# Transposes of query and key tiles in pairs at written places, one product group later

## The chip, the cores and the metric

One core of a Trainium2 chip runs the whole layer in one launch. The metric is the device time of an execution in microseconds. Before the change the median of three runs is 989.9 us (989.79 to 989.96). Five parts of the core matter here: TensorE multiplies matrices and transposes tiles; VectorE and ScalarE do elementwise work, and they alone take results out of PSUM, the memory that TensorE writes; GpSimd and SyncE issue transfers.

## The reference

One decoder layer on 256 tokens of width 2048. Three mixers work on one projection of the normed input and are joined by an output product; a gated feed-forward part follows. The change touches the second mixer, attention with low-rank queries and keys (8 heads, 128 plain and 64 rotary channels for each query and key, values of 128):

```python
q = (rms_norm(q_lat, g_q_lat) @ w_q_up).reshape(B, S, MLA_HEADS, MLA_QK_DIM)
kv = (rms_norm(kv_lat, g_kv_lat) @ w_kv_up).reshape(B, S, MLA_HEADS, MLA_NOPE_DIM + MLA_V_DIM)
k_nope, v = kv[..., :MLA_NOPE_DIM], kv[..., MLA_NOPE_DIM:]
...
q = rms_norm(q, g_q_mla)
k = rms_norm(k, g_k_mla)
q = jnp.concatenate([q[..., :MLA_NOPE_DIM], apply_rope(q[..., MLA_NOPE_DIM:], pos)], axis=-1)
k = jnp.concatenate([k[..., :MLA_NOPE_DIM], apply_rope(k[..., MLA_NOPE_DIM:], pos)], axis=-1)
o = causal_attention_blocks(q, k, v)
```

## The kernel before

Every fp32 operand of a large product is split into a rounded high part (ScalarE, L103, `wh`) and the rest (VectorE, L104, `wl`), and three products of these parts stand for one. The splits go through four buffers each, so a cast waits until TensorE has finished with the split four before it.

The stretch in question is the up-projection. `pool_in(g)` multiplies one group of the pooling mixer's channels, 48 matmuls of 256 columns (L134). `q_up(n)` gives the queries: n = 2 the rotary parts of all heads, n = 0 and 1 the plain parts of heads 0 to 3 and 4 to 7, 24 matmuls of 512 columns each (L185 to L187). `kv_up(0)` gives the keys in two halves of 12 such matmuls (h = 0: heads 0 to 3, h = 1: heads 4 to 7), `kv_up(1)` the values in two halves. These products have tokens on the partitions, in two tiles of 128 tokens (`tt`). The scores need features on the partitions, so each query or key tile (128 x 512) goes a way of its own: out of PSUM by ScalarE (L651 queries, L656 rotary queries, L686 keys) into a `tok` buffer of three; its squares and their sums (L272, L273) for the norm; for the rotary queries six operations of VectorE (L636 to L638); for the keys the norm's factor (L688, L212, L213, L691, L692) and a multiplication (L693); then `to_features`, four transposes on TensorE (L279) into a PSUM bank and a copy out of it (L283 and L287 on ScalarE, L285 on VectorE). Ten such tiles make ten sets of four transposes: two of rotary queries, four of keys, four of plain queries.

The code calls pool groups and up-projections in turn: `pool_in(0)`, `q_up(2)`, `pool_in(1)`, `kv_up(0)`, `pool_in(2)`, `q_up(0)`, `pool_in(3)`, `q_up(1)`, `kv_up(1)`. A scheduler then sets the order of instructions on every engine; only instructions given to `keep()` hold the order in which they are written among themselves. The transposes of L279 aren't given to it, so the scheduler puts them between the products where it takes them to be ready.

After that comes the output product (`out_part`), 24 matmuls of 512 columns a part, with steps of the attention in between: `mla_steps()` is called after every six matmuls (1.36 us at 0.227 us each) and counts its calls in `done[0]`. At call 1 the rotary keys are transposed (`rope_keys`, L727), at call 3 the pooling mixer's last product and the scores of heads 0 and 1 are made, and from call 6 on, every fourth call, the values of the head before, the turn of a head's probabilities (`turn`, three transposes, L495) and the scores of the head two further on (L742). Beside that, `first_jobs` makes sums of blocks of the down-projection's weights (subtractions L546 on VectorE, loads L539 and stores L548 by GpSimd).

Of the kernel before, what the change touches and what calls it, by code (L numbers as in the profile page):

```python
# [11 lines left out]
F32 = mybir.dt.float32  # L12
# [6 lines left out]
P = 128  # L19
# [4 lines left out]
H = 8  # L24
# [41 lines left out]
def layer(ctx, tc, xT_d, xn_d, memT_d, vec_d, tab_d, w_z_d, w_mqkr_d, w_q_d, w_kv_d, w_mem_d, w_pool_d, w_o_d,  # L66
          w_g_d, w_u_d, w_dn_d, out_d):
    nc = tc.nc
# [8 lines left out]
    def nm(s):  # L77
        uid[0] += 1
        return f"{s}_{uid[0]}"

    def ps_main():
        return psm.tile([P, 512], F32, tag="m", name=nm("psm"))

    def ps_aux():
        return psa.tile([P, 512], F32, tag="a", name=nm("psa"))

    def load_w(src, n, cut=STG, kept=False):
        raw = stage.tile([P, STG], F32, tag="wr", name=nm("wr"), bufs=3)
        for c in range(0, n, cut):
            keep(nc.sync.dma_start(raw[:, c:min(n, c + cut)], src[:, c:min(n, c + cut)]), kept)  # L90
        return raw[:]

    def keep(ins, on=True):

        return tc.keep_in_program_order(ins) if on else ins
# [45 lines left out]
    def gemm_z(ps, raw, act, between, low_first):  # L141


        nk = HS // P
        parts = [split_w(raw, c * HS, HS, shift=16 if c else 48) for c in range(KD // nk)]
        for low in ((True, False) if low_first else (False, True)):
            for k in range(KD):
                i = k % nk
                for a, m in enumerate(rounds(act, k, low)):
                    keep(nc.tensor.matmul(ps, parts[k // nk][low][:, i * P:(i + 1) * P], m,  # L150
                                          start=k + a == 0 and low == low_first,
                                          stop=k == KD - 1 and low != low_first, skip_group_check=True))
            if low == low_first:
                between()
# [62 lines left out]
    mp = mix.enter_context(tc.tile_pool(name="mix", bufs=1))  # L217

    identf = mp.tile([P, P], F32, name="identf")
# [11 lines left out]
    def sm(n):  # L231
        o = so[0]
        so[0] += n
        return small[:, o:o + n]

    def tok():
        return mp.tile([P, 512], F32, tag="tok", name=nm("tok"), bufs=3)
# [30 lines left out]
    def head_sq(dst, src):  # L268

        sq = mp.tile([P, 512], F32, tag="hsq", name=nm("hsq"), bufs=2)  # L270
        s3 = sq[:, :src.shape[1] * src.shape[2]].rearrange("p (h d) -> p h d", h=src.shape[1])
        nc.scalar.activation(s3, src, AF.Square)  # L272
        nc.vector.tensor_reduce(dst, s3, axis=AX.X, op=ALU.add)  # L273

    def to_features(dst, src, tt, n, scale=None, eng=None, bank=ps_aux):

        ps = bank()
        for i in range(n):
            nc.tensor.transpose(ps[:, i * P:(i + 1) * P], src[:, i * P:(i + 1) * P], identf[:])  # L279
        d = dst[:, :, tt * P:(tt + 1) * P]  # L280
        p3 = ps[:, :n * P].rearrange("p (i t) -> p i t", t=P)
        if scale is not None:
            nc.scalar.activation(d, p3, AF.Copy, scale=scale)  # L283
        elif eng == "v":
            nc.vector.tensor_copy(d, p3)  # L285
        else:
            nc.scalar.copy(d, p3)  # L287
# [29 lines left out]
    ps = ps_aux()  # L317
# [25 lines left out]
    for c in range(KD // 2):  # L343
# [10 lines left out]
        if c % 2:  # L354
            h = slice(2 * c - 2, 2 * c + 2)
# [5 lines left out]
    ps = ps_aux()  # L361
# [23 lines left out]
    gqk = sm(2)  # L385
# [137 lines left out]
    def mem_steps(m):  # L523
        if m == 0:
            mq_done()
        for h, step in beside.get(m, ()):
            (mem_heads[h].score, mem_heads[h].turn, mem_heads[h].values)[step]()
        if m == 6:
            latent_scales()
# [25 lines left out]
    for m in range(6):  # L555
        raw = load_w(w_z_d[m], STG)
        ps = ps_main()[:, 0:T]
        gemm_z(ps, raw, xg, lambda: mem_steps(m), m % 2 == 1)
        a = zs[:, m // 4, :]
        if m % 4 == 0:  # L560
            nc.scalar.activation(a, ps, AF.Square)
        else:
            t = mp.tile([P, T], F32, tag="zsq", name=nm("zsq"), bufs=2)
# [23 lines left out]
    def pool_in(g):  # L587
        raw = load_w(w_z_d[6 + g], STG)
        ps = ps_main()[:, 0:T]
        gemm_z(ps, raw, xg, lambda: mem_steps(6 + g), False) if g == 0 else gemm_t(ps, raw, 0, xg, range(KD))  # L590
        nc.vector.tensor_tensor(zp[:, g, :], ps, rxb[:], op=ALU.mult)
        if g % 2:
            keep(nc.sync.dma_start(x1n[:, g // 2, :], xn_d[g // 2]))
# [28 lines left out]
    qnT, knT, krT, qrT = qkv[:, 0:8], qkv[:, 8:16], qkv[:, 16:24], mqT  # L622
# [6 lines left out]
    def rotate(dst, src, s, tt, nh):  # L629
# [5 lines left out]
        for a, b, (ra, rb), op, o in ((x1, x2, (r[0], r[1]), ALU.subtract, 0), (x2, x1, (r[2], r[3]), ALU.add, 32)):  # L635
            nc.vector.tensor_tensor(t[:, 0], a, ra, op=ALU.mult)  # L636
            nc.vector.tensor_tensor(t[:, 1], b, rb, op=ALU.mult)
            nc.vector.tensor_tensor(dst[:, :, o:o + 32], t[:, 0], t[:, 1], op=op)  # L638

    def q_up(n):  # L640
        raw = load_w(w_q_d[n], STG)
        pss = [[ps_main()[:]] for _ in range(NT)]
        for i in range(2):
            hi, lo = split_w(raw, i * HS, HS)
            gemm_n(pss, hi.rearrange("p (k n) -> p k n", n=512), lo.rearrange("p (k n) -> p k n", n=512),
                   zl, 2 * i, i == 0, i == 1)
        for tt in range(NT):
            ps = pss[tt][0]
            t = tok()
            if n < 2:  # L650
                nc.scalar.copy(t[:], ps)  # L651
                head_sq(ssq_n[:, tt, 4 * n:4 * n + 4], t[:].rearrange("p (h d) -> p h d", d=NOPE))
                to_features(qnT[:, 4 * n:4 * n + 4], t, tt, 4, gqk[:, 0:1])
            else:
                t1 = tok()
                nc.scalar.copy(t1[:], ps)  # L656
                p3 = t1[:].rearrange("p (h d) -> p h d", d=ROPE)
                head_sq(ssq_r[:, tt, :], p3)
                rotate(t[:].rearrange("p (h d) -> p h d", d=ROPE), p3, 0, tt, H)
                to_features(qrT, t, tt, 4)  # L660

# [3 lines left out]
        head_sq(sskr[:, tt:tt + 1], kr[:, tt:tt + 1, :])  # L667
        rotate(krr[:, tt], kr[:, tt:tt + 1, :], 1, tt, 1)
    nc.vector.tensor_tensor(sskr, sskr, rx2, op=ALU.mult)
    def kv_up(n):  # L670
        raw = load_w(w_kv_d[n], STG)
        for h in range(2):
            pss = [[ps_main()[:]] for _ in range(NT)]
            hi, lo = split_w(raw, h * HS, HS)
            gemm_n(pss, hi.rearrange("p (k n) -> p k n", n=512), lo.rearrange("p (k n) -> p k n", n=512),
                   zl, 4, True, True)
            for tt in range(NT):
                ps = pss[tt][0]
                p3 = ps.rearrange("p (h d) -> p h d", d=128)
                if n == 1:  # L680
                    nc.scalar.activation(vv[:, tt, 4 * h:4 * h + 4, :], p3, AF.Copy, scale=skv[:, tt:tt + 1])
                    continue
                t = tok()
                t3 = t[:].rearrange("p (h d) -> p h d", d=NOPE)
                o = slice(tt * H + 4 * h, tt * H + 4 * h + 4)
                nc.scalar.copy(t[:], ps)  # L686
                head_sq(fk[:, o], t3)
                nc.vector.tensor_scalar(fk[:, o], fk[:, o], skv2[:, tt:tt + 1], sskr[:, tt:tt + 1],  # L688
                                        op0=ALU.mult, op1=ALU.add)
                rsqrt_(fk[:, o], fk[:, o], 1.0 / QK)  # L690
                nc.vector.tensor_scalar(fkn[:, o], fk[:, o], skv[:, tt:tt + 1], None, op0=ALU.mult)  # L691
                nc.vector.tensor_scalar(fkr[:, o], fk[:, o], rx[:, tt:tt + 1], None, op0=ALU.mult)  # L692
                nc.vector.tensor_tensor(t3, t3, fkn[:, o].unsqueeze(2).to_broadcast([P, 4, NOPE]), op=ALU.mult)  # L693
                to_features(knT[:, 4 * h:4 * h + 4], t, tt, 4, None, "v")


    pool_in(0)
    q_up(2)
    pool_in(1)
    kv_up(0)  # L700
    pool_in(2)
    q_up(0)
    pool_in(3)
    cat = mp.tile([P, KB, 2 * T], F32R, tag="cat", name="cat")
    pool_mix()
    q_up(1)

    fq = sm(NT * H)
    fq3 = fq.rearrange("p (t h) -> p t h", h=H)
# [4 lines left out]
    for tt in range(NT):  # L714
        nc.vector.tensor_scalar(fq3[:, tt], fq3[:, tt], sq_[:, tt:tt + 1], 1.0 / math.sqrt(QK),
                                op0=ALU.mult, op1=ALU.mult)

    kv_up(1)

    def rope_keys():  # L720
        for tt in range(NT):
# [24 lines left out]
    mla_heads = [mla_head(h) for h in range(H)]  # L746
    done = [0]

    def mla_steps():

        done[0] += 1
        if done[0] == 1:
            rope_keys()
        if done[0] == 3:
            pool_out()
            mla_heads[0].score()
            mla_heads[1].score()
        h, r = divmod(done[0] - 6, 4)
        if r == 0:
            if 0 < h < H:  # L760
                mla_heads[h - 1].values()
            if 0 <= h < H:
                mla_heads[h].turn()
            if 0 <= h < H - 2:
                mla_heads[h + 2].score()
        if done[0] == 4 * H + 4:
            mla_heads[H - 1].values()

# [163 lines left out]
    for f in range(1, KF):  # L932
        rows = [load_w(w[f], STG, kept=True) for w in (w_g_d, w_u_d)]
        behind = (lambda p=pss: glu(0, *p)) if f == 1 else None
# [4 lines left out]
        if f in job_at:  # L939
            now, n = job, job_at[f] + 1  # L940
# [110 lines left out]
    done = None  # L1051
    for c in range(2):
# [5 lines left out]
        for i, j in enumerate(ORDER):  # L1058
            kept = c > 0 or i > 1
# [16 lines left out]
        done = own  # L1076
# [85 lines left out]
```

## Time and profile before

| | |
|---|---|
| median of the runs | 989.9 us (989.79 to 989.96, 3 runs) |
| the profiled execution | 990.04 us, of which the span of instructions is 988.3 us |
| transposes at L279 into the banks of the attention | 48, mean 277 ns by the trace's modelled ends; 40 are the ten sets, 8 the memory mixer's queries |
| stretch of the ten tiles | about 132 to 176 us |

The views of the trace give, for each instruction or merged run of like instructions: its start, its length, engine, line, operation, out<-in by the program's names, shapes and number; in brackets the idle time of the engine before it and who ended it. On TensorE the ends are modelled and a matmul's row overlaps the next one's, so times between starts are what the engine really took.

### The profile page before, as it was taken

How to read it: one execution, taken by the hardware profiler on the slowest of the kernel's cores; microseconds unless marked ns; L12 is line 12 of the kernel's file. 1: busy time of each engine (PE TensorE's matmuls, PEld its weight loads, DVE VectorE, ACT ScalarE, POOL GpSimd, SP SyncE). 2: the span in 40 equal slices, each digit the busy share in tenths (PEclk: the TensorE clock that was granted, in tenths of full speed). 3: DMA queues.
4: the chain of work that ended last, by engine and by line, in shares of the span. 5: the costliest groups of instructions: out<-in, count | busy, mean ns of one | idle time of the engine just before them, and what ended most of it. 6: DMA issues, size and time to landing. Idle time of an engine off the chain costs nothing.

```text
span 988.3 us, 17435 instructions
## 1 busy us (share of the span) xinstructions
PE 982.9 (99%) x6858; PEld 911.1 (92%) x6858; DVE 801.1 (81%) x1261; ACT 580.4 (59%) x804; POOL 70.2 (7%) x136
## 2 busy tenths in 40 slices
PE   9999999999999999999999999999999999999998
PEld 8899988888889999999999999999999888888886
DVE  6868588888677788777977887878776899989997
ACT  6777665644376554455555545554545677757773
POOL 1100000011210101000100100101000000000000
PEclk9999999999999999999999999999999999999999
DMA  9865556689788988987898888979898899999993
GB/s 360 291 237 212 182 210 214 227 290 320 286 331 309 339 283 279 327 309 279 309 330 300 296 295 295 345 279 345 299 335 310 310 407 380 388 356 388 394 393 128
DMA packets 51730, 300.65 MB, mean 304 GB/s; under 512 B 5824, under 2 KB 6336, under 8 KB 25920
## 3 DMA queue, kind: packets, MB, share of 16 engines
q1 hardware_dynamic: 33984, 214.73, 59.5%
q0 software_dynamic: 17232, 84.03, 23.0%
q8 instruction: 53, 0.87, 0.3%
q10 hardware_dynamic: 432, 0.79, 0.3%
q14 instruction: 29, 0.24, 0.1%
HBM read 259.28 MB, written 40.24 MB: 303 GB/s over the span
## 4 chain that ended last, share of the span: by engine, by line
PE 98%; DVE 1%; ACT 0%; issue 0%
PE psm L169 47%; PE psm L185 5%; PE psm L186 5%; PE psm L187 5%; PE psm L150 4%; PE psa L967 4%; PE psa L966 4%; PE psa L965 4%; PE psm L967 4%; PE psm L966 4%; PE psm L965 4%; PE psm L134 2%; PE psa L742 1%; PE psa L185 1%; PE psa L187 1%; PE psa L186 1%
## 5 line engine op out<-in xcount | busy, mean ns | idle before, releaser
L104 DVE TENSOR_TENSOR wl<-wr,wh 128x1024 fp32r<-128x1024 f32 (+2 forms) x346 | 398.3, 1161 | 122.0 <-ACT wh L103 104.6
L103 ACT CAST wh<-wr 128x1024 fp32r<-128x1024 f32 (+2 forms) x346 | 343.9, 1002 | 167.6 <-PE psm L169 83.5
L169 PE MATMUL psm<-h,wh 128*128 128x256 f32 x2752 | 319.3, 276 | 0.0
L169 PEld LDWEIGHTS psm<-h,wh 128*128 128x128 f32 x2752 | 315.4, 188 | 0.0
L169 PE MATMUL psm<-h,wl 128*128 128x256 f32 x1376 | 163.1, 276 | 0.0
L169 PEld LDWEIGHTS psm<-h,wl 128*128 128x128 f32 x1376 | 159.3, 188 | 0.0
L875 ACT ACTIVATE gc<-psa,vec 128x256 f32<-128x256 f32 x44 | 24.9, 565 | 77.2 <-DVE psa L873 76.3
L546 DVE TENSOR_TENSOR wj<-wj 128x512 f32<-128x512 f32 x88 | 60.3, 685 | 1.1
L104 DVE TENSOR_TENSOR wl<-wj,wh 128x1024 fp32r<-128x1024 f32 (+1 forms) x50 | 53.6, 1091 | 5.1 <-PE psm L169 2.3
L103 ACT CAST wh<-wj 128x1024 fp32r<-128x1024 f32 (+1 forms) x50 | 47.0, 948 | 13.1 <-PE psm L966 6.7
L878 ACT ACTIVATE gc<-gc 128x256 f32<-128x256 f32 x44 | 18.4, 418 | 55.9 <-DVE gc L877 55.9
L103 ACT CAST wh<-dn 128x1024 fp32r<-128x1024 f32 (+1 forms) x40 | 39.1, 988 | 19.5 <-DVE dn L996 13.0
L104 DVE TENSOR_TENSOR wl<-dn,wh 128x1024 fp32r<-128x1024 f32 (+1 forms) x40 | 44.9, 1140 | 1.4 <-ACT wh L103 0.4
L877 DVE SCALAR_TENSOR_TENSOR gc<-psa,vec,gc 128x255 f32<-128x255 f32 x88 | 42.1, 479 | 1.5
L548 POOL DMA_DIRECT2D tsum<-wj x44 | 23.5, 534 | 222.4 <-DVE wj L546 199.2
L967 PE MATMUL psa<-wl,aS 128*128 128x512 f32 x98 | 38.3, 391 | 0.0
L967 PE MATMUL psm<-wl,aS 128*128 128x512 f32 x98 | 38.3, 390 | 0.0
L966 PE MATMUL psa<-wh,aS 128*128 128x512 f32 x98 | 38.2, 390 | 0.0
L965 PE MATMUL psm<-wh,aS 128*128 128x512 f32 x98 | 38.2, 389 | 0.0
L966 PE MATMUL psm<-wh,aS 128*128 128x512 f32 x98 | 38.2, 389 | 0.0
L965 PE MATMUL psa<-wh,aS 128*128 128x512 f32 x98 | 38.1, 389 | 0.0
L185 PE MATMUL psm<-wh,cat 128*128 128x512 f32 x96 | 38.1, 397 | 0.0
(262 smaller groups left out, 1477.9 us busy)
## 6 DMA issues: line engine op xcount, KB each, us to landing
wr<-in_w_g SPq DMA_DIRECT2D x44, 1024.0 KB, 6.8
wr<-in_w_u SPq DMA_DIRECT2D x44, 1024.0 KB, 6.9
wj<-in_w_dn POOLq DMA_DIRECT2D x22, 1024.0 KB, 6.8
tsum<-wj POOLq DMA_DIRECT2D x44, 512.0 KB, 6.8
wr<-in_w_o SPq DMA_DIRECT2D x16, 1024.0 KB, 7.3
wr<-tsum SPq DMA_DIRECT2D x15, 1024.0 KB, 7.5
wr<-in_w_dn SPq DMA_DIRECT2D x15, 768.0 KB, 7.8
wr<-in_w_z SPq DMA_DIRECT2D x10, 1024.0 KB, 5.0
```

The lines of the kernel that those rows point to most:

```text
L103: keep(nc.scalar.copy(hi[:, c:e], raw[:, o + c:o + e]), kept)
L104: keep(nc.vector.tensor_tensor(lo[:, c:e], raw[:, o + c:o + e], hi[:, c:e].bitcast(F32), op=ALU.subtract), kept)
L150: keep(nc.tensor.matmul(ps, parts[k // nk][low][:, i * P:(i + 1) * P], m, start=k + a == 0 and low == low_first, stop=k == KD - 1 and low ...
L169: nc.tensor.matmul(ps, parts[k // nk][low][:, i * P:(i + 1) * P], m, start=k + a == 0 and low == (s == 1), stop=k == KD - 1 and low == (s ...
L185: keep(nc.tensor.matmul(ps, xh, hi[:, i, o], start=first and i == 0, stop=False), kept)
L186: keep(nc.tensor.matmul(ps, xl, hi[:, i, o], start=False, stop=False), kept)
L187: keep(nc.tensor.matmul(ps, xh, lo[:, i, o], start=False, stop=last and i == nk - 1), kept)
L546: keep(nc.vector.tensor_tensor(r[:, d], r[:, a], r[:, b], op=ALU.subtract))
L877: nc.vector.scalar_tensor_tensor(gc[:, d:T], g[:, 0:T - d], v(w, f), gc[:, d:T], op0=ALU.mult, op1=ALU.add)
L965: nc.tensor.matmul(ps, a[0], b[0], start=first, stop=False)
L966: nc.tensor.matmul(ps, a[1], b[0], start=False, stop=False)
L967: nc.tensor.matmul(ps, a[0], b[1], start=False, stop=last)
```

## The change

The ten tiles are no longer transposed by the function that makes them. `q_up` and `kv_up` return lists of what is still to be transposed, and `turn_all` transposes the two token tiles of such a list one after the other, with `kept=True`, so that the transposes hold their written place among the other kept instructions and, with them, the products. The places are: rotary queries behind the second half of `kv_up(0)`; keys of heads 0 to 3 behind `pool_in(2)`; keys of heads 4 to 7 behind `q_up(0)`; queries of heads 0 to 3 behind `pool_in(3)`; queries of heads 4 to 7 behind the first half of `kv_up(1)`. Tiles that must live longer get buffers under the tags of the heads' probabilities, `p` and `pT` (two each, 128 x 512), by `held`. The first head's turn and the third head's scores move from call 6 of `mla_steps` to call 7.

```diff
-    def to_features(dst, src, tt, n, scale=None, eng=None, bank=ps_aux):
+    def to_features(dst, src, tt, n, scale=None, eng=None, bank=ps_aux, kept=False):
...
-            nc.tensor.transpose(ps[:, i * P:(i + 1) * P], src[:, i * P:(i + 1) * P], identf[:])
+            keep(nc.tensor.transpose(ps[:, i * P:(i + 1) * P], src[:, i * P:(i + 1) * P], identf[:]), kept)
...
+    def held(i):
+        return mp.tile([P, 512], F32, tag=("p", "pT")[i], name=nm("held"), bufs=2)
+
+    def turn_all(later):
+        for a in later:
+            to_features(*a, kept=True)
+
     def q_up(n):
...
+        later = []
         for tt in range(NT):
             ps = pss[tt][0]
-            t = tok()
+            t = held(n % 2)
...
-                to_features(qnT[:, 4 * n:4 * n + 4], t, tt, 4, gqk[:, 0:1])
+                later.append((qnT[:, 4 * n:4 * n + 4], t, tt, 4, gqk[:, 0:1]))
...
-                to_features(qrT, t, tt, 4)
+                later.append((qrT, t, tt, 4))
+        return later
...
-    def kv_up(n):
+    def kv_up(n, behind):
         raw = load_w(w_kv_d[n], STG)
+        out = []
...
+            if behind[h]:
+                turn_all(behind[h])
+            out.append([])
...
-                t = tok()
+                t = tok() if h else held(1)
...
-                to_features(knT[:, 4 * h:4 * h + 4], t, tt, 4, None, "v")
+                out[h].append((knT[:, 4 * h:4 * h + 4], t, tt, 4, None, "v"))
+        return out
...
     pool_in(0)
-    q_up(2)
+    turn_qr = q_up(2)
     pool_in(1)
-    kv_up(0)
+    turn_k = kv_up(0, (None, turn_qr))
     pool_in(2)
-    q_up(0)
+    turn_all(turn_k[0])
+    turn_q = q_up(0)
+    turn_all(turn_k[1])
     pool_in(3)
+    turn_all(turn_q)
...
-    q_up(1)
+    turn_q = q_up(1)
...
-    kv_up(1)
+    kv_up(1, (turn_q, None))
...
-            if 0 <= h < H:
+            if 0 < h < H:
                 mla_heads[h].turn()
-            if 0 <= h < H - 2:
+            if 0 < h < H - 2:
                 mla_heads[h + 2].score()
+        if done[0] == 7:
+            mla_heads[0].turn()
+            mla_heads[2].score()
```

What that does to the order on the engines, first on TensorE around the third pool product (L134, `psm_1713` before and `psm_1689` now). Before, both key tiles of heads 0 to 3 (`tok_1625`, `tok_1642`) are transposed inside it:

```order
L134 MATMUL psm_1713<-xg,wh_1714 128x256 x14
L279 MATMUL psa_1636<-identf,tok_1625 128x128 x4
L134 MATMUL psm_1713<-xg,wh_1714 128x256 x2
L134 MATMUL psm_1713<-xg,wl_1715 128x256 x8
L134 MATMUL psm_1713<-xg,wl_1743 128x256 x5
L279 MATMUL psa_1653<-identf,tok_1642 128x128 x4
L134 MATMUL psm_1713<-xg,wl_1743 128x256 x3
```

Now the rotary queries (`held_1506`, `held_1519`) stand ahead of it, and the same key tiles (`held_1613`, `held_1624`) behind it:

```order
L279 MATMUL psa_1653<-identf,held_1506 128x128 x4
L279 MATMUL psa_1659<-identf,held_1519 128x128 x4
L134 MATMUL psm_1689<-xg,wh_1690 128x256 x16
L134 MATMUL psm_1689<-xg,wl_1691 128x256 x8
L134 MATMUL psm_1689<-xg,wl_1719 128x256 x8
L134 MATMUL psm_1689<-xg,wh_1718 128x256 x16
L279 MATMUL psa_1747<-identf,held_1613 128x128 x4
L279 MATMUL psa_1753<-identf,held_1624 128x128 x4
```

The product runs through, and eight transposes follow it in one run.

Next on VectorE, the way to the last key tile, heads 4 to 7, second tokens (`tok_1694` before, `tok_1676` now). Before, from the scaling of the third pool product (L591) to that tile's multiplication (L693):

```order
L591 TENSOR_TENSOR zp<-psm_1713,rxb 128x256
L104 TENSOR_TENSOR wl_1833<-wr_1829,wh_1832 128x1024
L285 COPY qkv<-psa_1688 128x4x128
L213 RECIPROCAL small<-small 128x4
L104 TENSOR_TENSOR wl_1861<-wr_1829,wh_1860 128x1024
L691 TENSOR_SCALAR small<-small 128x4
L692 TENSOR_SCALAR small<-small 128x4
L693 TENSOR_TENSOR tok_1694<-tok_1694,small 128x512
```

Now, with the same lines under new numbers (L693 is L706, L691 and L692 are L704 and L705):

```order
L591 TENSOR_TENSOR zp<-psm_1689,rxb 128x256
L285 COPY qkv<-psa_1747 128x4x128
L213 RECIPROCAL small<-small 128x4
L285 COPY qkv<-psa_1753 128x4x128
L704 TENSOR_SCALAR small<-small 128x4
L705 TENSOR_SCALAR small<-small 128x4
L706 TENSOR_TENSOR tok_1676<-tok_1676,small 128x512
L104 TENSOR_TENSOR wl_1821<-wr_1817,wh_1820 128x1024
L104 TENSOR_TENSOR wl_1849<-wr_1817,wh_1848 128x1024
```

Two splits of the next pool group's weights moved behind the multiplication, and two copies of transposed keys, of heads 0 to 3, stand ahead of it, where one of heads 4 to 7 stood.

Last on TensorE, the first head's turn (L495). Before, between the products of one half of an output part (`wl_2130` is the last split of that half):

```order
L187 MATMUL psm_2126<-wl_2130,catm 128x512
L495 MATMUL psa_2145<-identf,p_2092 128x128 x3
L742 MATMUL psa_2151<-qkv 128x128
L742 MATMUL psa_2151<-qkv,mqT 128x128
L742 LDWEIGHTS identb
```

Now six products of the next half come first:

```order
L187 MATMUL psm_2126<-wl_2130,catm 128x512
L185 MATMUL psm_2125<-wh_2145,catm 128x512
L186 MATMUL psm_2125<-wh_2145,catm 128x512
L187 MATMUL psm_2125<-wl_2146,catm 128x512
L185 MATMUL psm_2126<-wh_2145,catm 128x512
L186 MATMUL psm_2126<-wh_2145,catm 128x512
L187 MATMUL psm_2126<-wl_2146,catm 128x512
L495 MATMUL psa_2155<-identf,p_2092 128x128 x3
```

The turn and the scores behind it moved as one.

## The prediction

> **What bounds the kernel now.** I read the page first, for the engine that fills the span; then the waits of TensorE; then the timeline of TensorE over the stretch that the diff touches, start by start.
>
> ```profile
> span 988.3 us, 17435 instructions
> PE 982.9 (99%) x6858; PEld 911.1 (92%) x6858; DVE 801.1 (81%) x1261; ACT 580.4 (59%) x804; POOL 70.2 (7%) x136
> PE 98%; DVE 1%; ACT 0%; issue 0%
> PE psa L279 <- DVE tok L638: 0.2, 1, 0.2
> PE psa L279 <- DVE small L213: 0.2, 1, 0.2
> ```
>
> The first three rows say that TensorE is the end-setter: busy for 982.9 of 988.3 us, and 98% of the chain that ended last. The next two are waits of TensorE at L279, the transposes that the change moves: 0.4 us in all by the waits view. So whatever TensorE saves reaches the end, and nothing saved elsewhere does. But 0.4 us is too little: matmul ends are modelled and overlap the next start, so a late start of up to some 0.16 us leaves no gap in that view. Starts must be compared with starts. This is what an undisturbed visit of four transposes looks like:
>
> ```profile
> 169.77 0.39 PE L185 MATMUL psm<-wh,zl 128*128 128x512 f32 x1
> 170.00 0.60 PE L279 MATMUL psa<-identf,tok 128*128 128x128 f32 x4
> 170.35 0.48 PE L186 MATMUL psm<-wh,zl 128*128 128x512 f32 x1
> 170.67 0.39 PE L187 MATMUL psm<-wl,zl 128*128 128x512 f32 x1
> ```
>
> A 512-wide product starts 0.227 us after the one before it (169.77 to 170.00). From 169.77 to 170.67 lie two products and the four transposes: 0.90 - 2 x 0.227 = 0.446 us for a clean visit, 0.35 of it up to the next product's start and 0.095 in that product. Now five of the other visits, and the first head's:
>
> ```profile
> 135.68 1.52 PE L134 MATMUL psm<-xg,wh 128*128 128x256 f32 x12
> 137.38 0.66 PE L279 MATMUL psa<-identf,tok 128*128 128x128 f32 x4 [0.18 <-DVE tok L638]
> 137.79 0.71 PE L134 MATMUL psm<-xg,wh 128*128 128x256 f32 x4
> ...
> 144.28 1.81 PE L134 MATMUL psm<-xg,wh 128*128 128x256 f32 x14
> ...
> 146.63 0.48 PE L134 MATMUL psm<-xg,wh 128*128 128x256 f32 x2
> 146.95 1.67 PE L134 MATMUL psm<-xg,wl 128*128 128x256 f32 x13
> ...
> 148.86 0.60 PE L134 MATMUL psm<-xg,wl 128*128 128x256 f32 x3
> ...
> 151.59 0.39 PE L187 MATMUL psm<-wl,zl 128*128 128x512 f32 x1
> ...
> 152.31 0.47 PE L185 MATMUL psm<-wh,zl 128*128 128x512 f32 x1
> ...
> 157.66 0.60 PE L279 MATMUL psa<-identf,tok 128*128 128x128 f32 x4
> 158.01 2.01 PE L134 MATMUL psm<-xg,wh 128*128 128x256 f32 x15
> ...
> 160.44 0.36 PE L134 MATMUL psm<-xg,wh 128*128 128x256 f32 x1
> ...
> 162.49 1.98 PE L134 MATMUL psm<-xg,wh 128*128 128x256 f32 x16
> 164.30 0.40 PE L185 MATMUL psm<-wh,zl 128*128 128x512 f32 x1
> ...
> 190.06 0.70 PE L495 MATMUL psa<-identf,p 128*128 128x128 f32 x3
> 190.60 0.39 PE L742 MATMUL psa<-qkv 128*128 128x128 f32 x2
> ...
> 198.28 0.49 PE L495 MATMUL psa<-identf,p 128*128 128x128 f32 x3
> 198.60 0.39 PE L742 MATMUL psa<-qkv 128*128 128x128 f32 x2
> ```
>
> A 256-wide product takes (164.30 - 162.49)/16 = 0.1135 us. Each visit is then late by what lies between the first and the last start less the products and the clean 0.35:
> - rotary queries, first token tile: 137.79 - 135.68 - 12 x 0.1135 - 0.35 = 0.40 us;
> - keys, heads 0 to 3, first: 146.63 - 144.28 - 14 x 0.1135 - 0.35 = 0.41; second: 148.86 - 146.95 - 13 x 0.1135 - 0.35 = 0.08;
> - keys, heads 4 to 7, first: 152.31 - 151.59 - 0.227 - 0.35 = 0.14;
> - queries of heads 0 to 3, second: 160.44 - 158.01 - 15 x 0.1135 - 0.35 - 0.095 (the product after the visit at 157.66) = 0.28;
> - the first head's turn of its probabilities (L495): 0.54 from start to start at 190.06 against 0.32 at 198.28, 0.22.
>
> The sum is **1.53 us**. The other four visits of L279 in this stretch cost the clean 0.446.
>
> **The change part by part.** Nothing is computed more or less: ten sets of four transposes and their ten copies out of PSUM stay, the ten tiles only live longer in other buffers. The costs are in the places.
>
> *The transposes themselves, eight in a row.* Five visits of eight replace ten of four. The trace has a visit of eight already:
>
> ```profile
> 177.29 0.40 PE L187 MATMUL psm<-wl,catm 128*128 128x512 f32 x1
> 177.52 1.04 PE L727 MATMUL psa<-identf,tok 128*128 128x128 f32 x8
> ...
> 178.63 0.39 PE L186 MATMUL psm<-wh,catm 128*128 128x512 f32 x1
> ...
> 180.94 0.40 PE L187 MATMUL psm<-wl,catm 128*128 128x512 f32 x1
> ```
>
> 178.63 - 177.29 - 2 x 0.227 = 0.886 us, against 2 x 0.446 = 0.892: pairing by itself saves nothing. Five pairs cost 4.43 us. Behind the eight the products keep 0.231 us (2.31 us for ten, 178.63 to 180.94), so the clock is not lowered by them. [...]
>
> *The waits that go.* A visit is late when its tile isn't ready. The new places come later, so I set each pair's new time beside the time at which the trace of before had its later tile ready. Taking out the two clean visits and the 0.40 that stand before 144.28 there, the new end of the first key-value product is 144.28 - 1.29 = 142.99; from there on, places follow by adding pairs (0.89) and products (48 x 0.1135 = 5.45; 24 x 0.227 = 5.44).
>
> ```profile
> 141.53 0.42 DVE L638 TENSOR_TENSOR tok<-rt 128x256 f32<-128x256 f32 x1
> 147.65 0.69 DVE L693 TENSOR_TENSOR tok<-tok,small 128x512 f32<-128x512 f32 x1
> 155.41 0.69 DVE L693 TENSOR_TENSOR tok<-tok,small 128x512 f32<-128x512 f32 x1
> 159.40 0.57 ACT L651 COPY tok<-psm 128x512 f32<-128x512 f32 x1
> 171.82 0.58 ACT L651 COPY tok<-psm 128x512 f32<-128x512 f32 x1
> ```
>
> - Rotary queries: place 142.99, ready 141.95. No wait.
> - First keys: place 142.99 + 0.89 + 5.45 = 149.33, second tile at 149.77; ready 148.34. No wait.
> - Second keys: place 149.33 + 0.89 + 5.44 = 155.66, second tile at 156.10; ready 156.10 by the old order. **The tightest place.** In the new order of VectorE two weight splits move behind that multiplication, and one more copy from PSUM comes ahead of it; at 1.2 and 0.69 us (rows below) it is ready some 1.7 us earlier, about 154.4. No wait.
> - Queries, heads 0 to 3: place 155.66 + 0.89 + 5.45 = 162.00, ready 159.97. No wait.
> - Queries, heads 4 to 7: place 162.00 + 0.89 + 5.44 + 2.72 = 171.05, second tile 171.49. The copy ended at 172.40; its product, which ended at 169.77, now ends at 168.33, so the copy ends by 170.96, and earlier if the copy of transposes (L283) ahead of it goes. Little room, no wait.
> - First head: its turn and the third head's scores (L495, then six matmuls and two masks) move behind six more products, 6 x 0.227 = 1.36 us later against a lateness of 0.22. No wait.
>
> ```profile
> 156.02 1.22 DVE L104 TENSOR_TENSOR wl<-wr,wh 128x1024 fp32r<-128x1024 f32 x1
> 157.16 0.69 DVE L285 COPY qkv<-psa 128x512 f32<-128x512 f32 x1
> ```
>
> *What the moves push back.* On VectorE the copies of a pair now wait for TensorE, with weight splits behind them: those of the third pool product stand behind the second keys. They end two splits after 154.4, at about 156.9; the first is needed sixteen products into that product, 155.66 + 0.89 + 1.82 = 158.4. So 2.8 us of cover for it, and every microsecond beyond is TensorE's. The subtractions of the w_down jobs (L546) fall behind the first heads' softmax, and with them GpSimd's stores of the sums and its next loads; SyncE's loads keep their order, with a buffer released about 1 to 2 us later. Their cover is in the waits of ScalarE:
>
> ```profile
> ACT wh L103 <- PE psm L169: 85.0, 123, 4.4
> ```
>
> ScalarE's weight casts wait for TensorE to free a buffer, not for loads: weights are ahead. I cost these moves at nothing; if the cover went, each microsecond of a late split would cost one.
>
> *The sum.* Bounds: nothing gained, if every wait comes back (0), and everything above clean work. Between 135.68 (the first visit's row) and 176.16, where the last key-value product ends, lie 40.48 us; 96 wide products, 112 narrow ones and ten visits are 21.79 + 12.71 + 4.46 = 38.96; the excess is 1.52, with the head's 0.22 at most 1.74. The 0.21 between 1.52 and the visits' 1.31 is products at 0.231 in place of 0.227 behind visits. Since a visit of eight shows the same 0.231, about half of it may go with half the visits; I leave it out of the sum and keep it for the range.
>
> ```profile
> 176.16 0.39 PE L185 MATMUL psm<-wh,catm 128*128 128x512 f32 x1
> ```
>
> I take 1.5 us of the 1.53: the profiled execution would fall from 990.04 (span 988.3 and 1.7 around it) to 988.5, and since the median of the runs, 989.90, lies 0.14 lower than that execution, to **988.4**. A measurement of this kernel tells about 0.2% from no change, 2.0 us: the forecast is a gain that counts as "same".
>
> **The rivals.**
> - *Waits in part.* The margins of 0.5 to 2 us were read from an order of VectorE and ScalarE that is gone. For it speaks that VectorE, which prepares every tile and every split, is busy 81%; against it that it does no more work than before. Half the gain gone: 989.1.
> - *Slower: the second keys turn into a wait.* Place: the multiplication of their second tile on VectorE. Price: ahead of the weight cast whose split precedes it, ScalarE now has one tile copy, one copy of transposes and one square more, 3 x 0.57 = 1.7 us, which takes the tile from 154.4 to 156.1, just in time. If VectorE in turn stands for ScalarE's roots of the norms as long again (1.7), and the two copies of the first keys (2 x 0.69) fall behind that wait and not into it, the tile is there at 159.2, and TensorE, due at 156.1, waits 3.1 us: 988.4 + 3.1 = 991.5. It decides from 157.6 on, where the wait has eaten the gain. Against it: VectorE has a split and reductions to do while it would wait. [...]
> - *Given back later*: TensorE arrives 1.5 us earlier and waits for weights or sums once. For it: the sums' stores and loads move. Against it: the 85.0 us above. 989.9.
> - *All the excess goes*, 1.74 us, and as much again as 0.3 at places that I don't see: below 987.9.
> - *It doesn't do what it says*: the order on TensorE shows the ten sets at the five places, so no.
>
> **How the numbers follow.** Forecast (gain of 1.0 to 1.9 us) 0.68; waits in part 0.15; given back 0.06; slower 0.06, more than half of it beyond 991.9 should the price be higher; more than all the excess 0.05. The range takes the forecast with the unknown cadence term, and most of the partial waits: 987.9 to 989.7. Faster by over 0.2% (under 987.9) 0.06, of which 0.05 is the last case and 0.01 the forecast's edge; slower (over 991.9) 0.04; within 0.90.
>
> **What would show it.** In the new timeline: no wait of TensorE at L279; each run of eight at 0.886; no L495 late by 0.2; values ending near 174.7 where it was 176.16, and later stages shifted by the same 1.4 to 1.5 us. Wrong: a bracketed wait at the second keys or at the last queries; or a shift that is there at 250 us and gone at the end.

## The result: 1000.0 us, 1% slower; the loss lies between 242 and 273 us

| | before | changed |
|---|---|---|
| median of the runs | 989.88 us (989.79 to 989.96, 4 runs) | 1000.01 us (998.93 to 1000.49, 4 runs) |
| ratio, 95% interval | | 1.0098 (1.0085 to 1.0110) |
| the profiled execution, its span | 990.04 us, 988.3 us | 1000.24 us, 998.5 us |
| shift of TensorE at 176 us | | 1.45 us earlier |
| shift at 238 us | | 1.69 us earlier |
| shift at the end of the span | | 10.2 us later |

The forecast was 988.4 us. The page of the changed kernel has TensorE still at 99%, but the chain that ended last goes through other engines now (PE was 98% of it):

```profile
PE 986.3 (99%) x6858; PEld 913.9 (92%) x6858; DVE 802.1 (80%) x1261; ACT 580.6 (58%) x804; POOL 70.2 (7%) x136
PE 73%; DMA 5%; issue 1%; DVE 1%; POOL 0%; ACT 0%; POOLq 0%; ACTq 0%; DVEq 0%
```

First the stretch that the diff aims at. TensorE's timeline in the changed kernel, from a product before the stretch to one at 236 us:

```profile
126.26 0.40 PE L185 MATMUL psm<-wh,zl 128*128 128x512 f32 x1
...
142.76 1.03 PE L279 MATMUL psa<-identf,held 128*128 128x128 f32 x8
143.55 1.19 PE L134 MATMUL psm<-xg,wh 128*128 128x256 f32 x8
...
171.07 1.03 PE L279 MATMUL psa<-identf,held 128*128 128x128 f32 x8
...
174.71 0.39 PE L185 MATMUL psm<-wh,catm 128*128 128x512 f32 x1
...
236.66 0.47 PE L185 MATMUL psm<-wh,catm 128*128 128x512 f32 x1
```

The same products (first and last of these) in the timeline of the kernel before:

```profile
126.47 0.40 PE L185 MATMUL psm<-wh,zl 128*128 128x512 f32 x1
...
238.35 0.47 PE L185 MATMUL psm<-wh,catm 128*128 128x512 f32 x1
```

The two executions are 0.21 us apart before the change begins (126.47 to 126.26). The pairs are visits of eight without a wait (the view of TensorE's waits has none at L279), and the gain is there: 176.16 - 174.71 - 0.21 = 1.24 us behind the last pair, 238.35 - 236.66 - 0.21 = 1.48 us behind the first head's turn. Then it is lost, eight times over. TensorE's timeline in the changed kernel again:

```profile
236.41 0.49 PE L495 MATMUL psa<-identf,p 128*128 128x128 f32 x3
...
242.00 0.39 PE L187 MATMUL psm<-wl,cat 128*128 128x512 f32 x1
244.65 0.99 PE L503 MATMUL psa<-pT,vv 128*128 128x256 f32 x2 [2.26 <-ACT pT L498]
...
261.90 0.39 PE L186 MATMUL psm<-wh,cat 128*128 128x512 f32 x1
267.17 0.80 PE L187 MATMUL psm<-wl,cat 128*128 128x512 f32 x1 [4.88 <-DVE wl L104]
267.76 0.63 PE L185 MATMUL psm<-wh,cat 128*128 128x512 f32 x1
268.19 0.63 PE L186 MATMUL psm<-wh,cat 128*128 128x512 f32 x1
```

Two waits, 244.65 - 242.00 - 0.23 = 2.42 us and 267.17 - 261.90 - 0.23 = 5.04 us, and behind each the products start 0.43 us apart instead of 0.23 for a while. The windows of the changed kernel (busy time and number of PE, PEld, DVE, ACT, POOL, then TensorE's granted clock, DMA share, GB/s) give a mean clock of 0.62 and 0.57 there, and shorter windows give 0.50, half the clock, from 246 to 248 and from 266 to 272 us. Before, it is 1.00 in all three:

```profile
244.50:249.00 4.50, 4.35 (x15) 3.67 (x16) 3.55 (x5) 2.74 (x5) 0.00 (x0) 0.62 0.86 289
249.00:265.00 16.00, 13.29 (x60) 10.71 (x58) 6.75 (x10) 3.43 (x4) 1.59 (x3) 1.00 0.98 362
265.00:273.00 8.00, 5.83 (x15) 4.63 (x16) 7.70 (x10) 4.27 (x7) 2.69 (x5) 0.57 0.67 222
```

The first slow stretch costs (1 - 0.62) x 4.5 = 1.7 us; the second, from 267.17 until products are 0.23 apart again at about 272.2, half of 5.0, 2.5 us. The sum, 2.42 + 5.04 + 1.7 + 2.5 = 11.7 us, is nearly the whole swing from 1.69 us ahead to 10.2 us behind (11.9). At 274.66, where the transposes of L858 start (264.70 before, there L838), TensorE is 9.96 us behind already.

What TensorE waited for leads back to the w_down jobs. VectorE's timeline in the changed kernel, ahead of each wait:

```profile
236.78 1.42 DVE L546 TENSOR_TENSOR wk<-wk 128x512 f32<-128x512 f32 x2 [3.31 <-DMA wk<-in_w_dn]
...
263.83 2.15 DVE L546 TENSOR_TENSOR wk<-wk 128x512 f32<-128x512 f32 x3 [9.04 <-DMA wk<-in_w_dn]
265.89 1.22 DVE L104 TENSOR_TENSOR wl<-wr,wh 128x1024 fp32r<-128x1024 f32 x1
```

At 263.83 VectorE had stood 9.04 us in front of a job's load. Behind that wait in its queue stood three subtractions and then the split (L104) that TensorE waited for until 267.17; the cast that the split needs had run on ScalarE at 254.73 (1.06 us).

The first wait took a longer way. At 236.78 VectorE had stood 3.31 us in front of a load, and a head's softmax stood behind it. From there ScalarE's queue carried it on, as its timeline in the changed kernel shows:

```profile
240.96 0.46 ACT L485 ACTIVATE p<-psa,st,small 128x128 f32<-128x128 f32 x1 [7.15 <-DVE st L483]
...
241.96 1.98 ACT L103 CAST wh<-wr 128x1024 fp32r<-128x1024 f32 x2
...
244.10 0.49 ACT L498 COPY pT<-psa 128x384 f32<-128x384 f32 x1
```

ScalarE stood 7.15 us in front of that softmax. The copy (L498) that TensorE waited for until 244.65 belongs to another head, whose probabilities TensorE had transposed at 236.41 already; it stood in the queue behind the softmax's exponentials (L485) and two casts.

The load that VectorE waited for was late because its predecessors were. The eight jobs share two buffers: GpSimd loads a block (L539), VectorE subtracts (L546), GpSimd stores two halves (L548), and the next load into that buffer waits for these stores. The jobs' subtractions in each kernel, from a window of 170 to 300 us (before, then changed; durations in ns, first and last start):

```profile
L546 DVE TENSOR_TENSOR wk<-wk x32: 672/691/695, 182.1 to 271.3; 128x512 f32<-128x512 f32 x32
```

```profile
L546 DVE TENSOR_TENSOR wk<-wk x32: 673/688/694, 194.7 to 277.1; 128x512 f32<-128x512 f32 x32
```

The first job's subtractions begin 12.6 us later (194.7 against 182.1). No data was missing: the first of GpSimd's loads was issued at 162.4, and VectorE waits for none ahead of 194.7. In the order of the changed kernel these subtractions simply stand behind the softmax of three heads. From there the chain that ended last in the changed kernel (176 to 300 us, start and length) goes round the buffers to TensorE:

```profile
205.71 7.95 DMA wk<-in_w_dn
...
230.41 11.23 DMA tsum<-wk
...
243.53 11.33 DMA tsum<-wk
...
255.42 8.39 DMA wk<-in_w_dn
...
265.89 1.23 DVE wl L104
267.17 0.80 PE psm L187
```

GpSimd's loads of the third and of the eighth job in its timeline, before and changed, show how little room these buffers have:

```profile
192.41 0.54 POOL L539 DMA_DIRECT2D wk<-in_w_dn  x1 [2.91 <-issue]
...
260.94 0.54 POOL L539 DMA_DIRECT2D wk<-in_w_dn  x1 [11.95 <-DMA tsum<-wk]
```

```profile
205.71 0.54 POOL L539 DMA_DIRECT2D wk<-in_w_dn  x1 [5.67 <-issue]
...
266.88 0.54 POOL L539 DMA_DIRECT2D wk<-in_w_dn  x1 [9.57 <-DMA tsum<-wk]
```

Five jobs took 68.5 us before (13.7 each) and 61.2 us when they were late (12.2 each). Of the 13.3 us of lateness 7.4 are made up by the eighth load.

### The profile page after: what moved, and what is told of

It reads as the page before. It is cut to its first block, busy times and chain, and to the rows that moved or that the text cites. A ratio compares the mean times of both kernels' runs of the same rounds, so it can differ in the third digit from the quotient of the medians.

```text
span 998.5 us, 17429 instructions
## 1 busy us (share of the span) xinstructions
PE 986.3 (99%) x6858; PEld 913.9 (92%) x6858; DVE 802.1 (80%) x1261; ACT 580.6 (58%) x804; POOL 70.2 (7%) x136
## 4 chain that ended last, share of the span: by engine, by line
PE 73%; DMA 5%; issue 1%; DVE 1%; POOL 0%; ACT 0%; POOLq 0%; ACTq 0%; DVEq 0%
PE psm L169 47%; PE psa L987 4%; PE psa L985 4%; PE psa L986 4%; PE psm L987 4%; PE psm L986 4%; PE psm L985 4%; DMA tsum<-wk 3%; DMA wk<-in_w_dn 2%; PE psm L134 1%; PE psm L187 1%; PE psm L185 1%; PE psm L186 1%; DVE wk L546 0%; PE psa L858 0%
## 5 line engine op out<-in xcount | busy, mean ns | idle before, releaser
L104 DVE TENSOR_TENSOR wl<-wr,wh 128x1024 fp32r<-128x1024 f32 (+2 forms) x346 | 398.7, 1162 | 117.2 <-ACT wh L103 99.5
L169 PE MATMUL psm<-h,wh 128*128 128x256 f32 x2752 | 319.3, 276 | 0.0
L169 PEld LDWEIGHTS psm<-h,wh 128*128 128x128 f32 x2752 | 315.4, 188 | 0.0
L169 PE MATMUL psm<-h,wl 128*128 128x256 f32 x1376 | 163.1, 276 | 0.0
L169 PEld LDWEIGHTS psm<-h,wl 128*128 128x128 f32 x1376 | 159.3, 188 | 0.0
L546 DVE TENSOR_TENSOR wj<-wj 128x512 f32<-128x512 f32 x88 | 60.4, 687 | 1.1
L104 DVE TENSOR_TENSOR wl<-wj,wh 128x1024 fp32r<-128x1024 f32 (+1 forms) x50 | 53.7, 1093 | 4.8 <-PE psm L169 2.3
L103 ACT CAST wh<-dn 128x1024 fp32r<-128x1024 f32 (+1 forms) x40 | 39.1, 989 | 19.5 <-DVE dn L1016 13.3
L104 DVE TENSOR_TENSOR wl<-dn,wh 128x1024 fp32r<-128x1024 f32 (+1 forms) x40 | 44.9, 1142 | 1.4 <-ACT wh L103 0.2
L187 PE MATMUL psm<-wl,cat 128*128 128x512 f32 x96 | 38.8, 404 | 4.9 <-DVE wl L104 4.9
L185 PE MATMUL psm<-wh,cat 128*128 128x512 f32 x96 | 39.6, 413 | 0.0
L186 PE MATMUL psm<-wh,cat 128*128 128x512 f32 x96 | 38.5, 401 | 0.0
L548 POOL DMA_DIRECT2D tsum<-wj x44 | 23.5, 534 | 213.2 <-DVE wj L546 193.3
L986 PE MATMUL psa<-wh,aS 128*128 128x512 f32 x98 | 38.2, 390 | 0.0
L986 PE MATMUL psm<-wh,aS 128*128 128x512 f32 x98 | 38.2, 390 | 0.0
```

The lines of the kernel that those rows point to most:

```text
L103: keep(nc.scalar.copy(hi[:, c:e], raw[:, o + c:o + e]), kept)
L104: keep(nc.vector.tensor_tensor(lo[:, c:e], raw[:, o + c:o + e], hi[:, c:e].bitcast(F32), op=ALU.subtract), kept)
L185: keep(nc.tensor.matmul(ps, xh, hi[:, i, o], start=first and i == 0, stop=False), kept)
L186: keep(nc.tensor.matmul(ps, xl, hi[:, i, o], start=False, stop=False), kept)
L187: keep(nc.tensor.matmul(ps, xh, lo[:, i, o], start=False, stop=last and i == nk - 1), kept)
L546: keep(nc.vector.tensor_tensor(r[:, d], r[:, a], r[:, b], op=ALU.subtract))
```

## The experiments

The theory (J in the expectations): moving the first head delays the first job, the two buffers stay late, and VectorE's queue carries the loads' lateness to TensorE (by way of ScalarE's queue at the first wait). The rivals: the pairs or the longer-lived tiles bring the loss (P), or only both parts together do (B).

| | time, us | ratio to before (95%) | first L546 at | TensorE's waits, 240 to 270 us |
|---|---|---|---|---|
| changed | 1000.01 | 1.0098 (1.0085 to 1.0110) | 194.7 | 2.3, 4.9 |
| e1 pairs alone | 988.60 | 0.9985 (0.9976 to 0.9994) | 180.5 | none |
| e2 head alone | 1001.30 | 1.0110 (1.0095 to 1.0126) | 196.0 | 2.6, 0.5, 5.6 |
| e3 job late alone | 1000.90 | 1.0108 (1.0094 to 1.0122) | 197.2 | 2.0, 0.6, 5.8 |
| e4 job early | 988.61 | 0.9986 (0.9977 to 0.9994) | 180.7 | none |
| e5 job between | 996.95 | 1.0068 (1.0053 to 1.0083) | 188.6 | 0.6, 0.9, 4.8 |
| e6 six jobs | 992.65 | 1.0024 (1.0013 to 1.0035) | 194.8 | 0.5, 2.7 |
| e7 jobs spread | 988.72 | 0.9990 (0.9980 to 0.9999) | 194.7 | none |
| e8 sums on GpSimd | 988.38 | 0.9984 (0.9974 to 0.9993) | 175.7 | none |
| e9 job ahead of the turn | 988.52 | 0.9980 (0.9970 to 0.9989) | 180.6 | none |
| e10 job behind the turn | 1000.12 | 1.0100 (1.0082 to 1.0118) | 194.7 | 2.0, 0.2, 5.6 |

**e1, the pairs alone.** The last part of the change is undone:

```diff
-            if 0 < h < H:
+            if 0 <= h < H:
                 mla_heads[h].turn()
-            if 0 < h < H - 2:
+            if 0 <= h < H - 2:
                 mla_heads[h + 2].score()
-        if done[0] == 7:
-            mla_heads[0].turn()
-            mla_heads[2].score()
```

> The change without its last part: the ten tiles are transposed in pairs at the new places, the first head's turn and the third head's scores stay at call 6. Theory J (moving the first head lets the first w_down job's subtractions start 12.5 us later, the two job buffers stay behind, and VectorE's queue carries their loads' lateness to TensorE): the first subtractions (L546) start near 181 us as before, no wait of TensorE near 244 and 267 us, the pairs' gain of 1.31 us stays to the end: 988.6 us. Rival P (the pairs, or the tiles held longer, bring the loss): first subtractions late or not, 999 to 1001 us. Rival B (only both parts together bring it): 988.6 us, so it isn't told from J by this run alone.

988.6 us, the gain of the pairs whole, the first subtractions at 180.5. P falls.

**e2, the head alone.** The kernel before with just those lines as the change has them.

> The kernel before with the last part of the change alone: the first head's turn and the third head's scores one call later, transposes of the ten tiles as before. Theory J: the first subtractions start near 196 us, TensorE waits some 2 and 5 us behind VectorE near 245 and 268 us and multiplies at half speed behind each wait: 989.9 - 0.2 + 11.7 = 1001.4 us, at least over 995. Rivals P and B: 989.7 us, no such waits.

1001.3 us, with waits like those of the changed kernel. B falls: the head's move alone costs all of it. One part was missed: half speed was expected behind each wait and came only behind the longest (see the last section).

**e3, the job late alone.** The kernel before; the first job is taken out of `first_jobs` and written at call 16 of `mla_steps`:

```diff
+        if done[0] == 16:
+            one_job()
...
+    def one_job():
+        i, raw = waiting.pop(0)
+        job_sums(i, raw)
+        if i + 2 < len(FIRST):
+            waiting.append(first_load(i + 2))
...
-        if parts[0] in FIRST:
-            i, raw = waiting.pop(0)
-            job_sums(i, raw)
-            if i + 2 < len(FIRST):
-                waiting.append(first_load(i + 2))
+        if parts[0] in FIRST[1:]:
+            one_job()
```

> The kernel before, with the first w_down job's subtractions, its stores and the next load into its buffer written eight calls later, and nothing else: neither pairs nor the first head are touched. By the order, the first subtractions then stand behind the third head's softmax, as in the changed kernel. Theory J: they start near 196 us, and the loss follows as in the changed kernel, 11 us or so: 998 to 1003 us. If the loss needs something else of the change (P, B, or the tiles' buffers p and pT held by the queries): 989.9 us within 1.

1000.9 us. Nothing of the change is in this kernel, and it has the change's loss: a late first job is enough.

**e4, the job early.** The whole change, with `one_job()` as in e3 but at call 2.

> The whole change, with the first w_down job's subtractions, its stores and the next load into its buffer written at call 2 and not after call 8. By the order they stand ahead of the first heads' score maxima. Theory J: first subtractions at about 180 us or earlier, no waits near 244 and 267 us, clock 1.00 there, and the forecast comes out: 988.2 to 988.5 us, 0.15% faster than the kernel before. Rivals P and B: the loss stays, 998 to 1001 us.

988.61 us, 0.11 us above the band expected. With an early first job the rest of the change loses nothing: in the changed kernel the late first job is needed for the loss.

**e5, the job between.** As e4, at call 4.

> The whole change, with the first w_down job's subtractions, stores and next load written at call 4: by the order they stand behind the softmax of heads 0 and 1 and ahead of the third head's. Theory J: the first subtractions start near 188 us, half of the lateness. In the kernel before the eight loads of the ring lie 13.7 us apart where the late ring shows it can do 12.2, so some 7 us of lateness are made up by the sixth load: 988.4 to 992 us. If any place behind the first heads' softmax brings the whole loss: 998 to 1001 us.

996.95 us: a miss. More was lost than I expected, because lateness grew on the way. GpSimd's timeline in e5 has the first job's second store and the load into its buffer, which by the program waits for that store (the view names no releaser there, only "issue"):

```profile
193.91 0.53 POOL L548 DMA_DIRECT2D tsum<-wk  x1 [2.00 <-DVE wk L546]
...
203.07 0.53 POOL L539 DMA_DIRECT2D wk<-in_w_dn  x1 [8.63 <-issue]
...
264.79 0.53 POOL L539 DMA_DIRECT2D wk<-in_w_dn  x1 [8.51 <-DMA tsum<-wk]
```

The same store in GpSimd's timeline of the kernel before:

```profile
188.97 0.53 POOL L548 DMA_DIRECT2D tsum<-wk  x1 [2.70 <-DVE wk L546]
```

In e5 the load came 203.07 - 193.91 = 9.2 us behind the store, before it was 192.41 - 188.97 = 3.4 us. So subtractions 6.5 us late made a load 10.7 us late, and after five jobs at 12.3 us each 3.9 us were left. Half of the delay brought most of the loss, and it isn't all or nothing either.

**e6, six jobs.** The changed kernel with `FIRST = (1, 3, 4, 6, 7, 9)`.

> The whole change, with six of the eight w_down jobs in this stretch; the last two blocks are summed in the feed-forward loop like the others there, so nothing is left out. The first job's subtractions stay late (194.7 us). Theory J: TensorE's wait of 2.3 us near 244.6 stays, the one of 4.9 us at 267 goes with the last two jobs, and the half-speed products behind it (some 2.2 us): 1000.0 - 7.1 = 993 us, if the two jobs cost nothing in the feed-forward loop; up to 998 if their eight subtractions (8 x 0.69 us) lie bare there. If the loss doesn't come by the ring's loads: 1000 us and more, the wait at 267 stays.

992.65 us, where 993 was expected: the wait at 267 us went with the last two jobs, the one near 244 stayed (2.67 us, up to 246.02).

**e7, jobs spread.** The changed kernel with `FIRST = (1, 3, 5, 7, 9, 11, 13, 15)`.

> The whole change, with the eight jobs' subtractions written behind every second weight group (1, 3, 5 ... 15) and not behind 1, 3, 4, 6, 7, 9, 10, 12: same work, the first subtractions as late as in the change (194.7 us), the ring as slow, but VectorE is asked for a job every 10.9 us, not every 7.5. Theory J (VectorE's queue stands behind a load that isn't there): the wait at 267 goes or shrinks to under 2 us, 989 to 994 us. If the late ring costs by itself (its transfers in the way of the weights'), wherever the subtractions stand: 998 us and more.

988.72 us, just below the band. This separates the late buffers from VectorE's queue. In e7 the first subtractions are as late as in the change and the last load is still later, as L546's source view and GpSimd's timeline show:

```profile
L546 DVE TENSOR_TENSOR wk<-wk x32: 681/686/694, 194.7 to 285.3; 128x512 f32<-128x512 f32 x32
```

```profile
272.56 0.53 POOL L539 DMA_DIRECT2D wk<-in_w_dn  x1 [12.28 <-DMA tsum<-wk]
```

The eighth load is issued at 272.56, against 266.88 in the change. Yet VectorE waits for wk 5.6 us in all instead of 19.5, TensorE doesn't wait in this stretch, and the clock is 1.00. The late transfers cost nothing here by themselves; what costs is a subtraction that stands in VectorE's queue before its load has landed.

**e8, sums on GpSimd.** The changed kernel; `first_jobs` calls `job_sums(i, raw, nc.gpsimd)`, and L546 uses that engine.

> The whole change, with the 32 subtractions of the eight jobs on GpSimd and not on VectorE (GpSimd issues these loads and stores as well, and does nothing else there). Theory J: a late load then holds GpSimd alone; VectorE's waits for wk are gone, and so are TensorE's near 244 and 267 us: 988.2 to 990 us, unless GpSimd's subtractions slow VectorE's or the ring gets so slow that its stores come late for the feed-forward part. If the ring's transfers themselves hold TensorE up: 998 us and more.

988.38 us. By itself it tells less than e7: the first job also starts earlier (175.7), since GpSimd has no softmax in its queue. It has a price on VectorE (last section).

**e9 and e10, the two sides of the turn.** The changed kernel, `one_job()` at call 7, once ahead of the first head's turn and once behind it:

```diff
+        if done[0] == 7:
+            one_job()
...
         if done[0] == 7:
             mla_heads[0].turn()
             mla_heads[2].score()
```

```diff
         if done[0] == 7:
             mla_heads[0].turn()
             mla_heads[2].score()
+            one_job()
```

> The whole change, with the first w_down job's subtractions, stores and next load written at call 7, directly ahead of the first head's turn, and not after call 8 behind it. By the order the four subtractions then stand among the first heads' score maxima, place for place as in the kernel before. Theory J: first subtractions near 181 us, no wait of TensorE behind VectorE near 244 and 267 us, clock 1.00 throughout, the forecast's gain: 988.2 to 988.6 us. If the first head's later turn costs anything beside the place of the subtractions: over 989.5 us.

> As e9, but the first job's subtractions are written at call 7 directly behind the first head's turn and the third head's scores, not ahead of them: two lines change places. By the order the subtractions fall behind the third head's softmax. Theory J: first subtractions near 194.7 us, TensorE's waits near 244 and 267 us and half-speed products behind at least one of them: 997 to 1002 us. If the call at which they are written decides, and not the side of the turn: as e9, 988.5 us.

988.52 and 1000.12 us: the same work, two lines exchanged, 11.6 us. VectorE's order of the first job beside the softmax of the first three heads (L487), with row numbers; first e9:

```
240 L546 TENSOR_TENSOR wk_2019<-wk_2019 128x512
...
253 L546 TENSOR_TENSOR wk_2019<-wk_2019 128x512
254 L487 RECIPROCAL st_2093<-st_2093 128x2
```

and e10:

```
250 L487 RECIPROCAL st_2093<-st_2093 128x2
...
260 L487 RECIPROCAL st_2169<-st_2169 128x2
263 L546 TENSOR_TENSOR wk_2019<-wk_2019 128x512
```

The head's later turn costs nothing by itself that these runs can tell. What decides is where the scheduler puts the first subtractions. How it chooses stays open: in the kernel before they are written behind the turn as well (after call 8, the turn at call 6) and come early, and written at call 4 (e5) they come later than at call 7 (e9).

## Why the prediction was wrong, step by step

- *What bounds the kernel, and the late starts*: right. The visits were to give 1.31 us and gave 1.24; with the head's 0.22 it was to be 1.53 and was 1.48.
- *Eight in a row*: right. 142.76 to 143.55 is 0.79 us to the next start; with the 0.095 in that product, 0.885 against 0.886 forecast.
- *The waits that go*: right. The first pair was placed at 142.99 and stood at 142.76, the last at 171.05 and 171.07; with the 0.21 us between the executions taken off, the first was on time and the last 0.23 us late. There was no wait at L279. The slower rival at the second keys, and waits in part, did not come about.
- *What the moves push back*: **the step that failed.** It named what happened ("The subtractions of the w_down jobs (L546) fall behind the first heads' softmax, and with them GpSimd's stores of the sums and its next loads") and then priced it: "I cost these moves at nothing". The cover quoted for it, ScalarE's casts waiting 85.0 us for TensorE, belongs to the weights' loads by SyncE, and to another stage: L169 is the feed-forward's product and runs from 301.8 to 769.9 us, after all that the change moves. It says nothing of the jobs' buffers, which GpSimd fills. Their rows stood in the waits view of the kernel before (170 to 300 us):

```profile
POOL wk L539 <- DMA tsum<-wk: 42.7, 4, 11.9
...
DVE wk L546 <- DMA wk<-in_w_dn: 9.0, 3, 5.2
```

  Four loads out of six waited for stores, up to 11.9 us, and VectorE already stood 9.0 us in front of late loads. These buffers had little room to make up 12.6 us. In the changed kernel the second row became:

```profile
DVE wk L546 <- DMA wk<-in_w_dn: 19.5, 5, 9.0
```

  The runs showed 11.7 us in place of nothing. The step also held that each microsecond of a late split would cost one. One of the two waits was for a late split (5.04 us), the other for a late copy of probabilities (2.42), and the slow clock behind them, which the step did not have, added 4.2.
- *Given back later* had the mechanism ("waits for weights or sums once") and a price of 1.5 us at most, the gain itself. Nothing bounds such a wait by the gain: the two waits took 7.5 us.
- *The order of an engine's queue* was weighed for a rival at another place (two copies of keys behind a wait of VectorE). It is what carried the loss here: VectorE's split at 265.89 stood behind three subtractions that had waited 9.04 us for a load that the split doesn't need, and ScalarE's copy at 244.10 behind a softmax that it doesn't need, in front of which ScalarE had stood 7.15 us.
- *The sum*: without the failed step, it stands. e9, the whole change with the first job where it was, takes 988.52 us against 988.4 forecast. The versions e1, e4, e7, e8 and e9 lie within 0.34 us of one another; all beat both kernels, and these runs can't rank them.

## What to carry to other kernels

When a change moves an instruction that refills a small set of buffers, read those buffers' own waits (who waits for the store, who for the load) and compare the pace at which they can turn with the pace asked of them; spare time in another engine's buffers is no cover. In VectorE's queue a subtraction that stood 9.04 us in front of a late load held the split behind it, and that split held TensorE for 5.04 us, so place such work when the load is surely there (e7), or make sure that the first job is early (e9). A gain of 1.5 us can be bought with a loss of nearly 12 us at a place 60 us further on, so follow how the order shifts on every engine, not only on the one that was edited.

## What the hardware showed that I had not expected

*Half speed behind short waits, in pieces of 3.4 us.* From the windows above, with 0.50 as the lowered clock, the array was at half clock for (1 - 0.62) x 2 x 4.5 = 3.4 us and (1 - 0.57) x 2 x 8 = 6.9 us, part of the second while it still waited (0.50 from 266 us on, the next product at 267.17). Reckoned in the same way, a window of 264 to 274 us gives 3.4 us in e5 (0.83) and 6.8 us in e2, e3 and e10 (0.66 each). Waits of nearly the same length fared differently. TensorE's timeline and a window of e2, then of e6:

```profile
246.36 0.70 PE L503 MATMUL psa<-pT,vv 128*128 128x256 f32 x2 [2.60 <-ACT pT L498]
```

```profile
246.00:250.00 4.00, 3.64 (x19) 3.12 (x20) 3.77 (x5) 2.85 (x5) 0.00 (x0) 1.00 0.90 298
```

```profile
246.02 1.22 PE L503 MATMUL psa<-pT,vv 128*128 128x256 f32 x2 [2.67 <-ACT pT L498]
```

```profile
246.00:250.00 4.00, 3.98 (x14) 3.43 (x15) 3.42 (x5) 2.61 (x4) 0.00 (x0) 0.63 0.87 303
```

2.60 us cost no clock, 2.67 us did, and so did the 2.26 us of the changed kernel. So the length of a wait alone doesn't tell whether the clock is lowered; what does, no run here shows.

*Slower splits on VectorE beside GpSimd's subtractions.* Groups of instructions from 176 to 280 us, kept apart by shape, in the kernel before and in e8 (busy us, mean ns):

```profile
L104 DVE TENSOR_TENSOR wl<-wr,wh 128x1024 fp32r<-128x1024 f32 x30 | 36.3, 1219 | 6.5 <-ACT wh L103 6.4
```

```profile
L546 POOL TENSOR_TENSOR wk<-wk 128x512 f32<-128x512 f32 x32 | 50.8, 1588 | 2.0
L104 DVE TENSOR_TENSOR wl<-wr,wh 128x1024 fp32r<-128x1024 f32 x30 | 46.2, 1559 | 14.2 <-ACT wh L103 13.9
```

With 32 subtractions on GpSimd (1588 ns each, against some 690 on VectorE), VectorE's 30 splits took 1559 ns on average instead of 1219, 10 us more in all, about half of the 22 us that the subtractions had taken there. TensorE didn't wait for it: the waits of e8 from 170 to 300 us have no row of TensorE.

*The time from a store to the load behind it varies.* Behind the same second store of the first job the next load came 3.4 us after the store's issue at 188.97 in the kernel before, and 9.2 us after 193.91 in e5. Why it differs was not tried.
